# Moving the first layer's activations by one 64-byte line against the weights, with alternating output groups

## The chip, the cores and the metric

The kernel runs on one core of one Trainium2 chip, in one launch. The metric is device time in microseconds (us), the median of several runs. One further execution was recorded by the hardware profiler; its page and trace are what the text reads. Engines are named as the profile names them: PE (matmuls), PEld (loading the stationary operand, the weights), DVE, ACT, POOL, and SP, which issues most DMAs.

## The reference, cut to what matters

A two-layer encoder over 272 tokens (16 learned ones and 256 of the input), 2048 channels wide. Nearly all of its time is in products of the activations with large float32 weight matrices:

```python
for i in range(DEPTH):                      # 2 layers
    h = _rmsnorm(h_stream, norm_mix[i])
    proj = h @ w_in[i]                      # q, k, v, f and the two gates
    ...                                     # attention, 2-D Fourier branch
    a_br = attn @ w_attn_br[i]
    s_br = fr.reshape(B, L, FOURIER_WIDTH) @ w_four[i]
    merged = g_attn * a_br + g_four * s_br
    h_stream = h_stream + merged @ w_out[i]
    h2 = _rmsnorm(h_stream, norm_ffn[i])
    up = h2 @ w_up[i]
    u_gate = _dwconv3_centred(up[..., :D_FF], w_conv[i], b_conv[i])
    u_val = up[..., D_FF:]
    h_stream = h_stream + (jax.nn.silu(u_gate) * u_val) @ w_down[i]
```

## The kernel before, in words

Activations lie transposed in on-chip memory: 128 channels on the partitions, the 272 tokens (`T`) along the row. A product is taken in two-part arithmetic. Each float32 number is split into a high part and a low part, the rest. For each block of 128x128 weights PE does three matmuls into the same accumulator:

- L372: high weights (`wh`) with high activations
- L373: the same `wh` with low activations
- L374: low weights (`wl`) with high activations

In the first layer each of these streams 272 columns, in the second most stream 258 (the first 14 tokens are no longer needed; k and v still take 272).

`group` (L352 on) makes 256 output channels as two accumulators in PSUM, `m` = 0 and 1 (the "two output groups"). Its weights come in chunks of 512 KB: four blocks of contraction (`c` = 0 to 3) by two blocks of output. A list `cm` holds the eight pairs (c, m) of a chunk. Unsorted, m changes fastest: each block of activations is used for m = 0, then for m = 1, and the two accumulators alternate. Sorted by m, the chunk's four blocks go to m = 0 first and then to m = 1. Before, the first layer sorts every chunk, and the second layer only the last chunk of a group. The very first groups, f0 and f1, have code of their own (`first_groups`, L415 on, matmuls L439 to L441), which always alternates m.

Weights go by DMA into `raw`, ACT rounds them to `wh` (L307), DVE takes the difference `wl` (L309), two chunks ahead of their use. Results leave PSUM through DVE and ACT. Four accumulators of tag "mm" exist, so that one group may be emptied while the next is computed.

**Addresses.** All of these are 4-byte words along one partition's row. Call 16 words (64 bytes) a line. A token row has 272 = 17 x 16 words, so that each next block of activations (kt) starts one line later, modulo four lines; and the weights' rows are 272 words apart too (`CS = T`), so that each next c also starts one line later. The distance between the weights of a block and its activations, modulo 64 words, is then the same for all c and kt. What sets it are the offsets in the table of constants (L64 to L69), added to the place of each tile in the program's memory map:

| operand | place of the tile, mod 64 | offset before | start before, mod 64 |
|---|---|---|---|
| weights `wh`, `wl`, c = 0 | 32 | | 32 |
| `xHL` layer 0, high / low | 32 | 11 / 7 | 43 / 39 |
| `gHL` (into w_down), high / low | 48 | 59 / 55 | 43 / 39 |
| `mH` / `mL` (into w_out) | 0 / 0 | 43 / 39 | 43 / 39 |
| `q1` / `q2` (attention's output), high / low | 48 / 40 | 59 / 63 | 43 / 39 |
| `xHL` layer 1, 258 columns, high / low | 32 | 61+14 / 57+14 | 43 / 39 |
| `xHL` layer 1, 272 columns (k and v), high / low | 32 | 61 / 57 | 29 / 25 |

So in the first layer the highs start 11 words into the line in which the weights of the same block start (both modulo four lines), and the lows 4 words before the highs. `LOW = 60` makes the low part's distance: 60 is 4 short of 64.

Which weights are loaded beside which stream matters below: while PE streams a matmul, the weights of the next one are loaded. Beside L372 that is `wh` again, for L373; beside L373 it is `wl` of the same block; beside L374 it is the next block's `wh`: the same c with the other m, or the next c.

Of the kernel before, what the change touches and what calls it, by code (L numbers as in the profile page):

```python
# [20 lines left out]
T = NM + SEQ  # L21
DEPTH = 2
KT = D // P
# [11 lines left out]
FF_SPLIT = (24, 20)  # L35
# [25 lines left out]
TAIL_ORDER = (2, 3, 0, 1)  # L61
F0 = 1536
CS = T
LOW = 60  # L64
X_PAD, X_AT = 192, (11, 61)
G_AT, G_PAD = 59, 128
M_AT, M_PAD = ((43, 39), (21, 17)), (60, 22)
Q_AT, Q_PAD = (((59,), (63,)), ((61, 45), (57, 57))), (((76,), (84,)), ((62, 46), (62, 62)))
A_PAD, O_AT = 48, 16  # L69

def _branch(text):
# [91 lines left out]
def encoder_kernel(ctx, tc, xT, params, consts, bmat, cfold, csign, w_fl, w_f64c, w_in, w_abr, w_four, w_f64, w_out, w_up, w_down, w_vn, w_dn, w_dt, out):  # L163
# [13 lines left out]
    for l in range(DEPTH):  # L177
        def g(w, mg, k0, k1):
            return [(w[l, mg, c], CW) for c in range(k0 // CW, k1 // CW)]
# [11 lines left out]
        for half in range(2):  # L191
            for kind, j in BRANCH_ORDER[half]:
                w, off, n = {"ga": (w_in, IN_GA, KT), "gf": (w_in, IN_GF, KT), "s": (w_four, 0, 8), "a": (w_abr, 0, 8)}[kind]
                chs = [(fw[KT + 2 * j + c], CW) for c in range(2)] if (l, kind) == (1, "s") else g(w, off + j, 0, n)
# [19 lines left out]
    def due(t):  # L214
        (t0, d0), (t1, d1) = next(v for v in zip(DUE, DUE[1:]) if v[0][0] <= t < v[1][0])
        return d0 + (d1 - d0) * (t - t0) // (t1 - t0)

    chunks, folded, streamed, mix, summed, stage, small_w = [], set(), set(), {}, {}, {}, {}
    t, done = 0, 0
    for key, chs in order:  # L220
        for j, ch in enumerate(chs):
            n = 0
            if key[0] == 1 and key[1] in ("t", "ug", "uv"):
                n = due(t) - done
# [57 lines left out]
    def pump(upto=None):  # L282
        if upto is None:
            if todo:
                todo.pop(0)[1]()
        while upto is not None and todo and todo[0][0] <= upto:
            todo.pop(0)[1]()
# [32 lines left out]
    def step(force=False):  # L320
        if not force and slow[1] and slow[2]:
            slow[0] -= 1
            if slow[0] <= 0:
                slow[0] = slow[2]
                if next(slow[1], None) is None:
                    slow[1] = None
        for s in shadow:
            s[0] -= 1
        for s in list(shadow):
            if force or s[0] <= 0:  # L330
                try:
                    s[0] = next(s[1])
                except StopIteration:
                    shadow.remove(s)
                return
# [9 lines left out]
    def next_split():  # L345
        i = st["next"]
        advance(i + 1 + LOOK)
        pump(i)
        st["next"] += 1
        return splits.pop(i)  # L350

    def group(key, rhs, width, tag="mm"):  # L352
        k, chs = order[st["grp"]]
        assert k == key, (k, key)
        st["grp"] += 1
        nm = "_".join(str(v) for v in key)
        ps = [psum.tile([P, 512], F32, tag=tag, name=f"ps_{nm}_{m}") for m in range(MG)]
        nk = CW * len(chs)
        for j in range(len(chs)):
            for _ in range(mix.get((key, j), 0)):  # L360
                next(st["products"])
            h, lo = next_split()
            cm = [(c, m) for c in range(CW) for m in range(MG)]
            if key[0] == 0 or j == len(chs) - 1:
                cm.sort(key=lambda v: v[1])
            for n, (c, m) in enumerate(cm):
                kt = CW * j + c
                x = rhs(kt)
                sl = slice(m * P, (m + 1) * P)
                o = ps[m][:, :width]  # L370
                a, b = x
                nc.tensor.matmul(o, h[:, c, sl], a, start=kt == 0, stop=False)  # L372
                nc.tensor.matmul(o, h[:, c, sl], b, start=False, stop=False)  # L373
                nc.tensor.matmul(o, lo[:, c, sl], a, start=False, stop=kt == nk - 1)  # L374
                if n % 2:
                    step()
                    pump()
        return ps
# [73 lines left out]

    XT = per.tile([P, KT, T], F32, name="XT")
    xf = per.tile([P, KT * 2 * T + X_PAD], F32R, name="xHL")
    xHLs = [xf[:, o:o + 2 * (KT * T + LOW)].rearrange("p (r x) -> p r x", r=2)[:, :, :KT * T].rearrange("p r (k t) -> p r k t", k=KT) for o in X_AT]
    xHL, xH, xL = xHLs[0], xHLs[0][:, 0], xHLs[0][:, 1]
    prm = per.tile([P, P_N], F32, name="prm")
    cst = per.tile([P, C_N], F32, name="cst")
# [71 lines left out]
    def norm_in(m, goff):  # L530
        norm_split(m, goff)
        norm_sum(m)
# [96 lines left out]
    for l in range(DEPTH):  # L629
# [7 lines left out]
        with tc.tile_pool(name=f"mix{l}", bufs=1) as mp:  # L637
# [105 lines left out]
            if l == 0:  # L743
# [19 lines left out]
                with tc.manual_schedule(engines={mybir.EngineType.PE, mybir.EngineType.DVE}):  # L763
                    ps = group((l, "f", 2), xr(0), T, "aux")
# [7 lines left out]
                tc.keep_in_program_order(nc.vector.tensor_tensor(br3[64:96], brem[32:64], br3[32:64].bitcast(F32), op=ALU.subtract))  # L772
                tc.keep_in_program_order(nc.vector.tensor_scalar(bgh, prm[:, P_BG:P_BG + DEPTH * 2 * KT], 0.5, None, op0=ALU.mult))
                f_evac(3, group((l, "f", 3), xr(0), T))
            else:
                push(norm_stats(hold), 8)
# [413 lines left out]
            for i in range(4):  # L1190
# [3 lines left out]
                if last:  # L1194
                    if i in (0, 2):
                        until(hold, "vt" if i == 0 else "fold")
                        for t_, n in ((qH, "q1"), (qL, "q2")):
                            o = Q_AT[l][t_ is qL][i // 2]
                            t = mp.tile([P, 4 * T + Q_PAD[l][t_ is qL][i // 2]], F32R, tag=n + "ab"[i // 2], name=n)
                            t_.append(t[:, o:o + 4 * T].rearrange("p (h t) -> p h t", t=T))  # L1200
                elif i == 0:
                    until(hold, "vt")
                    until(hold, "fold")
                    for t_, n in ((qH, "q1"), (qL, "q2")):
                        o = Q_AT[l][t_ is qL][0]
                        t = mp.tile([P, NH * T + Q_PAD[l][t_ is qL][0]], F32R, tag=n, name=n)[:, o:o + NH * T].rearrange("p (h t) -> p h t", t=T)
# [26 lines left out]
            for half in range(2):  # L1233
                mH = mL = None
                for n_, (kind, i) in enumerate(BRANCH_ORDER[half]):
                    if half or last and n_ >= 4:
                        slow[2] = 22
                    j = i - 4 * half
# [18 lines left out]
                    else:  # L1257
# [7 lines left out]
                        for m in range(MG):  # L1265
                            k = 2 * j + m
# [14 lines left out]
        with tc.tile_pool(name=f"ffn{l}", bufs=1) as fp:  # L1281
# [6 lines left out]
            def conv_gate(i):  # L1288
                ps = group((l, "ug", i), xr(lo), W)
                until(hold, "tok2")  # L1290
                cs = []
                for m in range(MG):
                    mt = 2 * i + m
                    wc = lambda t: prm[:, P_CW + (l * 3 + t) * FT + mt:P_CW + (l * 3 + t) * FT + mt + 1]
                    bc = prm[:, P_CB + l * FT + mt:P_CB + l * FT + mt + 1]
                    u = fp.tile([P, T], F32, tag="u", name="u", bufs=3)
                    nc.vector.tensor_tensor(u[:, lo:T], ps[m][:, :W], rstdB[:, lo:T], op=ALU.mult)
                    cv = fp.tile([P, T], F32, tag="cv", name="cv", bufs=4)
                    nc.scalar.activation(cv[:, lo2:T], u[:, lo2:T], AF.Identity, bias=bc, scale=wc(1))
                    a = max(lo2, 1)  # L1300
                    nc.vector.scalar_tensor_tensor(cv[:, a:T], u[:, a - 1:T - 1], wc(0), cv[:, a:T], op0=ALU.mult, op1=ALU.add)
                    nc.vector.scalar_tensor_tensor(cv[:, lo2:T - 1], u[:, lo2 + 1:T], wc(2), cv[:, lo2:T - 1], op0=ALU.mult, op1=ALU.add)
                    nc.scalar.activation(cv[:, lo2:T], cv[:, lo2:T], AF.Silu)
                    if not last:
                        nc.vector.tensor_tensor(cv, cv, rstdB, op=ALU.mult)
                    cs.append(cv)
                return cs

            def split_to(h, low, v):
                nc.scalar.copy(h, v)  # L1310
                nc.vector.tensor_tensor(low, v, h.bitcast(F32), op=ALU.subtract)

            k0 = 0
            for c, n in enumerate(() if last else FF_SPLIT):
                gf = fp.tile([P, FF_SPLIT[0] * 2 * T + G_PAD], F32R, tag="gHL", name="gHL")
                gH, gL = (gf[:, G_AT + (FF_SPLIT[0] * T + LOW) * r:G_AT + (FF_SPLIT[0] * T + LOW) * r + FF_SPLIT[0] * T].rearrange("p (k t) -> p k t", t=T) for r in range(2))
                for i in range(k0 // MG, (k0 + n) // MG):
                    cs = conv_gate(i)
                    ps = group((l, "uv", i), xr(0), T)
                    for m in range(MG):  # L1320
                        j = 2 * i + m - k0
                        nc.vector.tensor_tensor(cs[m], cs[m], ps[m][:, :T], op=ALU.mult)
                        split_to(gH[:, j], gL[:, j], cs[m])
                for mg in range(8):
                    ps = group((l, "d", c, mg), lambda kt: (gH[:, kt], gL[:, kt]), T)
                    for m in range(MG):
                        mt = 2 * mg + m
                        nc.vector.tensor_tensor(XT[:, mt], XT[:, mt], ps[m][:, :T], op=ALU.add)
                        if c == len(FF_SPLIT) - 1:
                            norm_in(mt, P_NM + (l + 1) * KT)  # L1330
                k0 += n
            if last:
# [152 lines left out]
                for i in UP_ORDER:  # L1485
# [16 lines left out]
                    for m in range(0 if i in VPAIRS else MG):  # L1502
                        j = 2 * i + m
# [19 lines left out]
                for b in TAIL_ORDER:  # L1523
                    k, chs = order[st["grp"]]
# [95 lines left out]
```

## Time and profile before

| | us |
|---|---|
| median of 3 runs | 2483.73 (2483.13 to 2485.19) |
| the profiled execution | 2484.18 |
| its span, first to last instruction | 2482.4 |
| layer 0 (to the first k group of layer 1) | 0 to 1301.3 |
| of that, w_in, attention, Fourier branch and w_out | 0 to 522.6 |
| of that, w_up and w_down | 522.6 to 1301.3 |

The time of the profiled execution is 1.8 us above its span, and 0.45 us above the median. On the page, PE and PEld are two parts of one engine that overlap; matmuls are pipelined, so that the record of one lasts more than twice as long as the step from its start to the next one's start. Where speed is meant, the steps are to be read, not the records' lengths.

### The profile page before, as it was taken

How to read it: one execution, taken by the hardware profiler on the slowest of the kernel's cores; microseconds unless marked ns; L12 is line 12 of the kernel's file. 1: busy time of each engine (PE TensorE's matmuls, PEld its weight loads, DVE VectorE, ACT ScalarE, POOL GpSimd, SP SyncE). 2: the span in 40 equal slices, each digit the busy share in tenths (PEclk: the TensorE clock that was granted, in tenths of full speed). 3: DMA queues.
4: the chain of work that ended last, by engine and by line, in shares of the span. 5: the costliest groups of instructions: out<-in, count | busy, mean ns of one | idle time of the engine just before them, and what ended most of it. 6: DMA issues, size and time to landing. Idle time of an engine off the chain costs nothing.

```text
span 2482.4 us, 48288 instructions
## 1 busy us (share of the span) xinstructions
PE 2473.8 (100%) x19040; PEld 2401.3 (97%) x19040; DVE 1984.1 (80%) x3143; ACT 1335.9 (54%) x1901; POOL 205.0 (8%) x394
## 2 busy tenths in 40 slices
PE   9999999999999999999999999999999999999999
PEld 9999999999999999999999999999998899988987
DVE  7687866778878767888778887666878787898898
ACT  5455534554444334444445655444676665676665
POOL 0000000012212222222210000000000000000000
PEclk9999999999999999999999999999999999999999
DMA  7545557879999999999986647888888887888887
GB/s 249 170 154 165 192 195 245 271 256 376 403 326 387 404 386 385 395 384 396 396 296 201 198 159 245 271 266 274 254 271 296 299 291 237 264 283 296 281 303 271
DMA packets 194805, 706.88 MB, mean 285 GB/s; under 512 B 22145, under 2 KB 27393, under 8 KB 194321
## 3 DMA queue, kind: packets, MB, share of 16 engines
q1 hardware_dynamic: 146768, 517.09, 60.3%
q0 software_dynamic: 46368, 184.57, 21.3%
q8 instruction: 149, 2.44, 0.4%
q10 hardware_dynamic: 1440, 2.13, 0.2%
q14 instruction: 80, 0.65, 0.1%
HBM read 623.32 MB, written 111.15 MB: 296 GB/s over the span
## 4 chain that ended last, share of the span: by engine, by line
PE 99%; DMA 0%; DVE 0%; issue 0%; ACT 0%; POOL 0%; DVEq 0%; ACTq 0%; POOLq 0%
PE ps_p L1462 14%; PE ps_ug L372 7%; PE ps_ug L374 7%; PE ps_ug L373 7%; PE ps_uv L372 4%; PE ps_uv L374 4%; PE ps_uv L373 4%; PE ps_d L372 4%; PE ps_d L374 3%; PE ps_d L373 3%; PE ps_gf L372 3%; PE ps_ga L372 2%; PE ps_o L372 2%; PE ps_ga L374 2%; PE ps_gf L374 2%; PE ps_o L374 2%
## 5 line engine op out<-in xcount | busy, mean ns | idle before, releaser
L307 ACT CAST wh<-raw 128x1024 fp32r<-128x1024 f32 (+1 forms) x961 | 997.7, 1043 | 873.1 <-PE ps_ug L373 211.6
L309 DVE TENSOR_TENSOR wl<-raw,wh 128x1024 fp32r<-128x1024 f32 (+1 forms) x961 | 1158.6, 1218 | 386.2 <-ACT wh L307 375.1
L372 PE MATMUL ps_ug<-xHL,wh 128*128 128x272 f32 (+1 forms) x1408 | 397.9, 283 | 0.0
L374 PE MATMUL ps_ug<-xHL,wl 128*128 128x272 f32 (+1 forms) x1408 | 394.3, 281 | 0.2 <-DVE wl L309 0.2
L373 PE MATMUL ps_ug<-xHL,wh 128*128 128x272 f32 (+1 forms) x1408 | 394.5, 280 | 0.0
L373 PEld LDWEIGHTS ps_ug<-xHL,wh 128*128 128x128 f32 x1408 | 264.8, 188 | 3.2
L372 PEld LDWEIGHTS ps_ug<-xHL,wh 128*128 128x128 f32 x1408 | 264.3, 188 | 3.3
L374 PEld LDWEIGHTS ps_ug<-xHL,wl 128*128 128x128 f32 x1408 | 263.7, 188 | 1.5 <-DVE wl L309 1.1
L372 PE MATMUL ps_uv<-xHL,wh 128*128 128x272 f32 (+1 forms) x896 | 254.9, 285 | 0.0
L374 PE MATMUL ps_uv<-xHL,wl 128*128 128x272 f32 (+1 forms) x896 | 252.2, 282 | 0.3 <-DVE wl L309 0.3
L373 PE MATMUL ps_uv<-xHL,wh 128*128 128x272 f32 (+1 forms) x896 | 252.5, 282 | 0.0
L1462 PE MATMUL ps_p<-wh,opnd 128*128 128x512 f32 x816 | 221.8, 393 | 0.0
L372 PE MATMUL ps_d<-gHL,wh 128*128 128x272 f32 x704 | 201.3, 286 | 0.0
L373 PE MATMUL ps_d<-gHL,wh 128*128 128x272 f32 x704 | 199.2, 283 | 0.0
L374 PE MATMUL ps_d<-gHL,wl 128*128 128x272 f32 x704 | 198.9, 283 | 0.0
L1462 PEld LDWEIGHTS ps_p<-wh,opnd 128*128 128x128 f32 x816 | 148.1, 188 | 28.6
L373 PEld LDWEIGHTS ps_uv<-xHL,wh 128*128 128x128 f32 x896 | 168.9, 188 | 0.8
L374 PEld LDWEIGHTS ps_uv<-xHL,wl 128*128 128x128 f32 x896 | 168.0, 188 | 1.0 <-DVE wl L309 1.0
L372 PEld LDWEIGHTS ps_uv<-xHL,wh 128*128 128x128 f32 x896 | 168.2, 188 | 0.8
L535 DVE TENSOR_TENSOR wi<-wi,wi 128x512 f32<-128x512 f32 x224 | 147.2, 685 | 0.1
L372 PE MATMUL ps_ga<-xHL,wh 128*128 128x272 f32 (+1 forms) x512 | 146.5, 286 | 0.0
L372 PE MATMUL ps_gf<-xHL,wh 128*128 128x272 f32 (+1 forms) x512 | 145.4, 284 | 0.0
(375 smaller groups left out, 5776.1 us busy)
## 6 DMA issues: line engine op xcount, KB each, us to landing
raw<-in_w_up SPq DMA_DIRECT2D x288, 512.0 KB, 6.6
raw<-in_w_in SPq DMA_DIRECT2D x191, 512.0 KB, 4.2
raw<-in_w_down SPq DMA_DIRECT2D x88, 512.0 KB, 7.2
wi<-in_w_dn POOLq DMA_DIRECT2D x80, 512.0 KB, 9.7
ft<-wi POOLq DMA_DIRECT2D x80, 512.0 KB, 7.8
raw<-ft SPq DMA_DIRECT2D x80, 512.0 KB, 4.7
raw<-in_w_out SPq DMA_DIRECT2D x64, 512.0 KB, 4.4
raw<-fv SPq DMA_DIRECT2D x64, 512.0 KB, 4.7
```

The lines of the kernel that those rows point to most:

```text
L307: nc.scalar.copy(h[:, a:b], r[:, a:b])
L309: nc.vector.tensor_tensor(lo[:, a:b], r[:, a:b], h[:, a:b].bitcast(F32), op=ALU.subtract)
L372: nc.tensor.matmul(o, h[:, c, sl], a, start=kt == 0, stop=False)
L373: nc.tensor.matmul(o, h[:, c, sl], b, start=False, stop=False)
L374: nc.tensor.matmul(o, lo[:, c, sl], a, start=False, stop=kt == nk - 1)
L535: tt = lambda *v, **kw: tc.keep_in_program_order(nc.vector.tensor_tensor(*v, **kw))
L1462: nc.tensor.matmul(ps[h], x, w[:, 512 * h:512 * h + 512], start=fresh and (s_, q) in BEGIN and first, stop=(s_, q) in END and end, skip_gr ...
```

## The change

Two things, in the first layer alone. (1) The high activations start one line earlier (27 instead of 43, modulo 64), so that the weights of the same block start in the line after them, 5 words on; the lows start 4 words after the highs (31) instead of 4 before. This holds for all four kinds of operand, `xHL`, `gHL`, `mH`/`mL` and `q1`/`q2`. (2) `group` doesn't sort a chunk in the first layer any more, not the last one either: the two accumulators alternate in every chunk. The second layer keeps its addresses and its order.

```diff
-LOW = 60
-X_PAD, X_AT = 192, (11, 61)
-G_AT, G_PAD = 59, 128
-M_AT, M_PAD = ((43, 39), (21, 17)), (60, 22)
-Q_AT, Q_PAD = (((59,), (63,)), ((61, 45), (57, 57))), (((76,), (84,)), ((62, 46), (62, 62)))
+LOW = (4, 60)
+X_PAD, X_AT = 192, (59, 61)
+G_AT, G_PAD = 43, 128
+M_AT, M_PAD = ((27, 31), (21, 17)), (60, 22)
+Q_AT, Q_PAD = (((43,), (55,)), ((61, 45), (57, 57))), (((76,), (84,)), ((62, 46), (62, 62)))
...
-            if key[0] == 0 or j == len(chs) - 1:
+            if key[0] == 1 and j == len(chs) - 1:
                 cm.sort(key=lambda v: v[1])
...
-    xHLs = [xf[:, o:o + 2 * (KT * T + LOW)].rearrange("p (r x) -> p r x", r=2)[:, :, :KT * T].rearrange("p r (k t) -> p r k t", k=KT) for o in X_AT]
+    xHLs = [xf[:, o:o + 2 * (KT * T + n)].rearrange("p (r x) -> p r x", r=2)[:, :, :KT * T].rearrange("p r (k t) -> p r k t", k=KT) for o, n in zip(X_AT, LOW)]
...
-                gH, gL = (gf[:, G_AT + (FF_SPLIT[0] * T + LOW) * r:G_AT + (FF_SPLIT[0] * T + LOW) * r + FF_SPLIT[0] * T].rearrange("p (k t) -> p k t", t=T) for r in range(2))
+                gH, gL = (gf[:, G_AT + (FF_SPLIT[0] * T + LOW[0]) * r:G_AT + (FF_SPLIT[0] * T + LOW[0]) * r + FF_SPLIT[0] * T].rearrange("p (k t) -> p k t", t=T) for r in range(2))
```

On PE, the first chunk of the first w_down group (tiles `ps_d_0_0` and `ps_d_0_1` are its accumulators m = 0 and 1, three rows to a block). Before:

```order
L372 MATMUL ps_d_0_0_10286<-gHL,wh_10223 128x272
L373 MATMUL ps_d_0_0_10286<-gHL,wh_10223 128x272
L374 MATMUL ps_d_0_0_10286<-gHL,wl_10224 128x272
L372 MATMUL ps_d_0_0_10286<-gHL,wh_10223 128x272
L373 MATMUL ps_d_0_0_10286<-gHL,wh_10223 128x272
L374 MATMUL ps_d_0_0_10286<-gHL,wl_10224 128x272
```

and now, at the same place:

```order
L372 MATMUL ps_d_0_0_10286<-gHL,wh_10223 128x272
L373 MATMUL ps_d_0_0_10286<-gHL,wh_10223 128x272
L374 MATMUL ps_d_0_0_10286<-gHL,wl_10224 128x272
L372 MATMUL ps_d_0_1_10287<-gHL,wh_10223 128x272
L373 MATMUL ps_d_0_1_10287<-gHL,wh_10223 128x272
L374 MATMUL ps_d_0_1_10287<-gHL,wl_10224 128x272
```

Before, the accumulator stays m = 0 for the chunk's four blocks of contraction; now it changes after every third matmul, and the weights loaded beside L374 are every other time those for m = 1 of the same c. The count of matmuls is the same.

On DVE, the last group of attention's output projection (a7) and the start of the second half of w_out (`ps_o`): L1268 and L1269 take `ps_a` out of PSUM and add the other branch, L1271 writes `mL`, which the w_out group reads. Before:

```order
L309 TENSOR_TENSOR wl_6092<-raw_5907,wh_6091 128x4x256
L1268 SCALAR_TENSOR_TENSOR th<-th,ps_a_0_6048 128x272
L1269 TENSOR_TENSOR th<-th 128x272
L1268 SCALAR_TENSOR_TENSOR th<-th,ps_a_1_6049 128x272
L1269 TENSOR_TENSOR th<-th 128x272
L309 TENSOR_TENSOR wl_6132<-raw_5940,wh_6131 128x4x256
L1271 TENSOR_TENSOR mL<-th,mH 128x272 x2
```

and now:

```order
L309 TENSOR_TENSOR wl_6092<-raw_5907,wh_6091 128x4x256
L1268 SCALAR_TENSOR_TENSOR th<-th,ps_a_0_6048 128x272
L1268 SCALAR_TENSOR_TENSOR th<-th,ps_a_1_6049 128x272
L1269 TENSOR_TENSOR th<-th 128x272 x2
L309 TENSOR_TENSOR wl_6132<-raw_5940,wh_6131 128x4x256
L1271 TENSOR_TENSOR mL<-th,mH 128x272 x2
```

The same instructions stand there; only the two halves of the emptying are interleaved, because both accumulators now become ready at nearly the same time. POOL's and SP's rows are the same as before.

## The prediction

> **What bounds the kernel now.** I read the page first: busy shares, and the chain that ended last.
>
> ```profile
> span 2482.4 us, 48288 instructions
> PE 2473.8 (100%) x19040; PEld 2401.3 (97%) x19040; DVE 1984.1 (80%) x3143; ACT 1335.9 (54%) x1901; POOL 205.0 (8%) x394
> ...
> PE 99%; DMA 0%; DVE 0%; issue 0%; ACT 0%; POOL 0%; DVEq 0%; ACTq 0%; POOLq 0%
> ```
>
> PE is never free and the chain is PE from end to end. Next, what PE waited for:
>
> ```profile
> engine line waited for: us in total, times, longest us
> PE ps_f L439 <- ACT wh L307: 4.4, 1, 4.4
> PE ps_uv L374 <- DVE wl L309: 0.3, 1, 0.3
> PE ps_ug L374 <- DVE wl L309: 0.2, 1, 0.2
> ```
>
> These are 4.9 us in all, so nothing is to be had from waits. The time is a count of matmuls times the step from one start to the next. The count of the first layer, from the windows view of line L372 up to layer 1, and of L439:
>
> ```profile
> 0.00:1301.30 1301.30, 937.74 (x3264) 612.88 (x3265) 1.00 0.84 306
> ...
> 0.00:1301.30 1301.30, 19.91 (x64) 13.03 (x64) 1.00 0.84 306
> ```
>
> That is 3,328 triples (L372 to L374, or L439 to L441), 9,984 matmuls of 272 columns. One nanosecond on each is 10 us, and a whole 0.2% of the time, about what a measurement of this kernel can tell from no change, is 5.0 us or 0.5 ns on each. The clock in these rows is 1.00, so no throttle hides in the step.
>
> **The step, and what it depends on.** The first half of w_down, groups by line, then one row of the tile view with first and last start:
>
> ```profile
> L372 PE MATMUL ps_d<-gHL,wh 128*128 128x272 f32 x384 | 109.8, 286 | 0.0
> L373 PE MATMUL ps_d<-gHL,wh 128*128 128x272 f32 x384 | 108.7, 283 | 0.0
> L374 PE MATMUL ps_d<-gHL,wl 128*128 128x272 f32 x384 | 108.5, 283 | 0.0
> ...
> L374 PE MATMUL ps_d<-gHL,wl x384: 282/283/283, 806.6 to 947.6; 128*128 128x272 f32 x192
> ```
>
> From 806.6 to 947.6 lie 383 triples: 368.1 ns a triple, 122.7 ns a step. The three records are 285.9, 283.1 and 282.6 ns (busy by count), 851.6 together; so a record is 161.1 ns longer than its step on average ((851.6 - 368.1) / 3), and with that constant the steps are 124.8, 122.0 and 121.5. The matmuls are alike but for the addresses, so the kinds must differ by what is read beside them. The timeline shows it: the next weights are loaded from the moment a stream starts.
>
> ```profile
> 899.99 0.28 PE L373 MATMUL ps_d<-gHL,wh 128*128 128x272 f32 x1
> 899.99 0.19 PEld L374 LDWEIGHTS ps_d<-gHL,wl 128*128 128x128 f32 x1
> ...
> 900.11 0.28 PE L374 MATMUL ps_d<-gHL,wl 128*128 128x272 f32 x1
> 900.12 0.19 PEld L372 LDWEIGHTS ps_d<-gHL,wh 128*128 128x128 f32 x1
> ```
>
> Beside L372 the weights start in the same line as the highs (modulo four lines): the dear kind, 285.9. Beside L374, in the sorted order, they are the next c's, one line further, 5 words past the start of the highs: the cheap kind, 282.6. That both stand at third place as well is seen in f0 and f1, which alternate at the same addresses, so that L441 has the same line every other time:
>
> ```profile
> L441 PE MATMUL ps_f<-xHL,wl x33: 282/286/392, 19.8 to 31.9; 128*128 128x272 f32 x33
> L439 PE MATMUL ps_f<-xHL,wh x32: 285/286/286, 19.9 to 31.7; 128*128 128x272 f32 x32
> L440 PE MATMUL ps_f<-xHL,wh x32: 283/283/286, 20.1 to 31.8; 128*128 128x272 f32 x32
> ```
>
> L441 is 282 or 286: same line 286, one line on 282, at the same place in the triple and with the same stream. This is the pair on which the forecast rests.
>
> **The change part by part.** *Highs one line back.* Beside L372 the weights now start one line on, 5 words past the highs, as they did beside L374. Its record should go from 285.9 to 282.6: -3.3 ns a triple.
>
> *Alternation.* Beside L374 the weights are half the time the same c's: again 5 words on, 282.6, no change. Half the time they are the next c's, now two lines on. No row of 272 columns shows that distance. Its bounds are the two kinds seen, 282.6 and 285.9; no row is nearer to the one than to the other, since same line and two lines lie one line to either side of the cheap place; I take the dear one: +3.3 ns in half the triples, +1.7 a triple. With the cheap one it would be 0, another 5.7 us off the sum (1.7 x 3,328).
>
> *Lows.* No row shows the new distance, 1 word, either. Put the loaded weights at word 32 in each case: the streams seen then start at 27 (L374, 282.6), 39 (L373, 283.1) and 43 (L372, 285.9), all at word 3 of a group of four, as the new lows are. The new start, 31, lies between the first two. The bounds are 282.6 (-0.5) and 285.9 (+2.8); I take 283.1, no change.
>
> *Sum.* -3.3 + 1.7 + 0 = -1.6 ns a triple; times 3,328 is **-5.3 us**. All of it is on the path, since PE sets the end. The two unknown places together reach from -1.6 - 1.7 - 0.5 = -3.8 ns a triple (-12.6 us) to -1.6 + 2.8 = +1.2 ns (+4.0 us).
>
> *The later accumulator.* Without sorting, m = 0 is ready 9 matmuls or 1.1 us later (9 x 0.1227), near the group's end. The tightest place is a7 into w_out:
>
> ```profile
> L373 PE MATMUL ps_o<-mL,wh x40: 283/283/283, 475.6 to 490.0; 128*128 128x272 f32 x40
> ...
> 474.89 0.43 DVE L1268 SCALAR_TENSOR_TENSOR th<-th,ps_a 128x272 f32<-128x272 f32 x1
> ...
> 477.79 0.79 DVE L1271 TENSOR_TENSOR mL<-th,mH 128x272 fp32r<-128x272 f32 x2
> ...
> 479.30 0.28 PE L373 MATMUL ps_o<-mL,wh 128*128 128x272 f32 x1
> ```
>
> The two `mL` are done at about 478.2 and 478.6; the first reader of the first is the L373 at 479.30 (third block of the second chunk), 1.1 us later. w_out's first L373 stands at 475.6, so a7 ended near 475.5; its m = 0 had ended 1.5 us before that (12 steps), but DVE took it up only at 474.89. Now it can do so near 475.3, 0.4 us later. The reader moves by more: in alternating order the third block of a chunk stands after 12 matmuls, not 6, 0.74 us later. So cost 0; the cover is the chunk that stands between. If it were gone, each of some six hand-overs (f, q, a twice, the two w_down) would lose up to 1.1 us, 6.6 us.
>
> **A rule of the skill against it.** In the Trainium skill, "TensorE: Matmul & The Clock Gate", section "Step-by-step: what each phase is for", says that PE has two independent read ports, and that loading the next weights takes no bandwidth from the running matmul. By that, relative addresses could not matter and the sum would be 0. The 282 and 286 of L441 speak against it, and more so the k rows below, where the same three lines step by 129 ns.
>
> **The rivals.**
>
> *No gain (slightly slower).* The lows pay: 1 word past their start may collide where 5 words don't. At 285.9 they cost +2.8 ns, the sum becomes +1.2 ns a triple, +4.0 us: 2487.7. It decides from 284.7, where the gain is used up. For it: 1 word is nearer than any seen; against it: its place between two cheap starts. Chance 0.19.
>
> *Two free ports.* If the 3 ns had another cause than the addresses, such as the repeated `wh`, distance would be free, the triple would stay at 368.1, and the time at 2483.7. Against it stands L441. Chance 0.04. (It is what the rule above of the Trainium skill's "TensorE: Matmul & The Clock Gate" would give.)
>
> *Not the distance, but the change of block (slower).* Where L441 is cheap, the next stream is another block of activations, too; where it is dear, the next one reads the same block again. If that is the cause, L372 stays at 285.9, L374 becomes dear in half the triples, and a dear third matmul also makes a following L440 dear (283 to 286 in its row). The price stands in f0 and f1, which run just so:
>
> ```profile
> 24.15 0.28 PE L441 MATMUL ps_f<-xHL,wl 128*128 128x272 f32 x1
> ...
> 27.86 0.28 PE L441 MATMUL ps_f<-xHL,wl 128*128 128x272 f32 x1
> ```
>
> 30 steps in 3.71 us, 123.7 ns against 122.7: 1.0 ns on 9,792 matmuls (f0 and f1 have it already), +9.8 us, 2493.5. It decides if L372 stays above some 284 ns, where what it saves no longer pays for the alternation (285.9 - 1.7). Against it: L372's own next stream is another one, the lows, and it is dear. Chance 0.13.
>
> *The streams lose their phase.* In layer 1, k and v read 272 columns from 29 and 25, which also puts the weights in the next line, 3 and 7 words on:
>
> ```profile
> 1303.79 0.29 PE L373 MATMUL ps_k<-xHL,wh 128*128 128x272 f32 x1
> ...
> 1305.99 0.29 PE L372 MATMUL ps_k<-xHL,wh 128*128 128x272 f32 x1
> ```
>
> 17 steps in 2.20 us, 129.4 ns: 6.7 ns dearer, +67 us over 9,984 matmuls, 2550. By line alone this is the nearest place to the new one. Against it: these starts are word 1 of a 16-byte group, while all well-running ones, and the new ones, are word 3. Chance 0.11.
>
> *All cheap.* Every record at 282.6 is -3.8 ns a triple, -12.6 us: 2471.1. The second layer agrees roughly:
>
> ```profile
> L374 PE MATMUL ps_o<-mH,wl x126: 276/277/278, 1588.5 to 1632.0; 128*128 128x258 f32 x126
> ...
> L1541 PE MATMUL ps_t<-wh,t 128*128 128x512 f32 x56 | 17.1, 390 | 0.0
> ...
> L1541 PE MATMUL ps_t<-wh,t 128*128 128x256 f32 x8 | 1.6, 281 | 0.0
> ```
>
> 125 triples in 43.5 us are 116.0 ns a step at 258 columns; a column costs (390 - 281) / 256 = 0.43 ns, so 14 more make 122.0, -0.7 ns on 9,984, -7 us. Chance 0.18.
>
> That the change doesn't do what it says is excluded: PE's rows alternate in every first-layer group, and the starts follow from the offsets.
>
> **How the numbers follow.** The execution profiled took 2484.18, 0.45 over the median; -5.3 gives 2478.9 in its own time and **2478.4** as a median. The forecast (-8 to -3 us, 2475.5 to 2480.5) has 0.35, of which 0.06 lies within 5.0 us of the old time. Faster by over 0.2%: 0.29 + 0.18 = 0.47. Within: 0.06 + 0.19 + 0.04 = 0.29. Slower: 0.13 + 0.11 = 0.24. The range reaches from the cheapest sum, 2471, rounded out to 2470 for the ends of that case, to 2494, which takes in the change of block; it leaves out the lost phase (0.11) and some hundredths at the low end.
>
> **What would show it.** L372 of `ps_d` at 282 to 283 instead of 286: the high step right; at 286, distance is not what counts. L374 with two values, 282 and 286: the alternation as reckoned; one value of 282: the cheap rival. L373 tells the lows: 283, or 286. The first half of w_down, 141 us from first to last start, should take 140.4; 142 is the change of block, 149 the lost phase. Records spread over many values are the lost phase too. A PE wait on `mL`, `gL` or `xHL` would make the hand-over wrong. Layer 1 should keep its 1,181 us.

## The result and the profile after

| | median of 9 runs, us | profiled execution, us | its span, us |
|---|---|---|---|
| before | 2484.29 (2483.12 to 2485.31) | 2484.18 | 2482.4 |
| after | 2490.86 (2489.92 to 2493.01) | 2493.01 | 2491.2 |

After / before is 1.0027, 95% interval 1.0017 to 1.0038: **slower by 6.6 us**, where 5.3 us less was forecast. The page of the kernel after, busy times and the chain that ended last:

```profile
span 2491.2 us, 48303 instructions
PE 2481.9 (100%) x19040; PEld 2409.8 (97%) x19040; DVE 1983.0 (80%) x3143; ACT 1335.1 (54%) x1901; POOL 203.4 (8%) x394
...
PE 99%; DMA 0%; DVE 0%; issue 0%; ACT 0%; POOL 0%; DVEq 0%; ACTq 0%; POOLq 0%
```

The bound is the same, and so is the count of matmuls. PE's waits after:

```profile
PE ps_f L439 <- ACT wh L307: 5.1, 2, 4.4
PE ps_uv L374 <- DVE wl L309: 0.3, 1, 0.3
PE ps_ug L374 <- DVE wl L309: 0.2, 1, 0.2
```

No new wait has come, so the time is again count by step. Where the first layer grew is read from the tile view's first and last starts: the first k matmul and the last one of w_down. Before, then after:

```profile
L372 PE MATMUL ps_k<-xHL,wh x64: 286/288/491, 59.5 to 1314.1; 128*128 128x272 f32 x64
L374 PE MATMUL ps_d<-gHL,wl x704: 282/283/283, 806.6 to 1301.2; 128*128 128x272 f32 x176
```

```profile
L372 PE MATMUL ps_k<-xHL,wh x64: 283/288/491, 61.5 to 1322.8; 128*128 128x272 f32 x64
L374 PE MATMUL ps_d<-gHL,wl x704: 283/283/288, 811.9 to 1309.9; 128*128 128x272 f32 x176
```

From 59.5 to 1301.2 are 1241.7 us; from 61.5 to 1309.9 are 1248.4. These +6.7 us are as much as the medians differ (6.6); the other 2.0 us of the profiled execution lie ahead of the first k matmul, in the opening stretch, where the first k matmul stood anywhere from 58.3 to 60.3 us in the kernels below. Behind the last w_down row nothing changed (2482.4 - 1301.2 = 1181.2; 2491.2 - 1309.9 = 1181.3). The first half of w_down, grouped by line (busy us, mean ns), and then in the tile view (shortest, median, longest; first and last start):

```profile
L373 PE MATMUL ps_d<-gHL,wh 128*128 128x272 f32 x384 | 109.7, 286 | 0.0
L372 PE MATMUL ps_d<-gHL,wh 128*128 128x272 f32 x384 | 109.6, 285 | 0.0
L374 PE MATMUL ps_d<-gHL,wl 128*128 128x272 f32 x384 | 108.7, 283 | 0.0
```

```profile
L372 PE MATMUL ps_d<-gHL,wh x384: 283/284/287, 811.7 to 953.7; 128*128 128x272 f32 x192
L373 PE MATMUL ps_d<-gHL,wh x384: 284/284/288, 811.8 to 953.8; 128*128 128x272 f32 x192
L374 PE MATMUL ps_d<-gHL,wl x384: 283/283/288, 811.9 to 953.9; 128*128 128x272 f32 x192
```

From 811.9 to 953.9 are 142.0 us, against 141.0 before and 140.4 forecast: 370.8 ns a triple against 368.1. (Below, a triple's price is the mean over a stage, taken from the starts in the trace to the nanosecond and good to some 0.1 ns; such rows check it roughly.) L372's record fell only from 285.9 to 285.4 ns, and L373's rose from 283.1 to 285.7. L374, which was to carry the price of the alternation, rose by half a nanosecond. The timeline shows why:

```profile
899.79 0.28 PE L374 MATMUL ps_d<-gHL,wl 128*128 128x272 f32 x1
899.92 0.29 PE L372 MATMUL ps_d<-gHL,wh 128*128 128x272 f32 x1
900.04 0.29 PE L373 MATMUL ps_d<-gHL,wh 128*128 128x272 f32 x1
900.17 0.28 PE L374 MATMUL ps_d<-gHL,wl 128*128 128x272 f32 x1
900.29 0.28 PE L372 MATMUL ps_d<-gHL,wh 128*128 128x272 f32 x1
900.41 0.28 PE L373 MATMUL ps_d<-gHL,wh 128*128 128x272 f32 x1
900.54 0.28 PE L374 MATMUL ps_d<-gHL,wl 128*128 128x272 f32 x1
```

The load beside the L374 at 899.79 is the next c's, two lines on: its own record is short, and the L372 and L373 behind it are long. The load beside the one at 900.17 is the same c's, 5 words on, and the next two are short. L372 has the same pair of addresses in both places and two prices. **A step is not set by its own pair alone.**

### The profile page after: what moved, and what is told of

It is laid out like the page before. It is cut to its first block, busy times and chain, and to the rows that moved or that the text cites. A ratio compares the mean times of both kernels' runs of the same rounds, so it can differ in the third digit from the quotient of the medians.

```text
span 2491.2 us, 48303 instructions
## 1 busy us (share of the span) xinstructions
PE 2481.9 (100%) x19040; PEld 2409.8 (97%) x19040; DVE 1983.0 (80%) x3143; ACT 1335.1 (54%) x1901; POOL 203.4 (8%) x394
## 4 chain that ended last, share of the span: by engine, by line
PE 99%; DMA 0%; DVE 0%; issue 0%; ACT 0%; POOL 0%; DVEq 0%; ACTq 0%; POOLq 0%
PE ps_p L1462 14%; PE ps_ug L372 7%; PE ps_ug L374 7%; PE ps_ug L373 7%; PE ps_uv L372 4%; PE ps_uv L373 4%; PE ps_uv L374 4%; PE ps_d L372 4%; PE ps_d L373 4%; PE ps_d L374 3%; PE ps_gf L372 2%; PE ps_ga L372 2%; PE ps_o L372 2%; PE ps_o L373 2%; PE ps_gf L373 2%; PE ps_ga L373 2%
## 5 line engine op out<-in xcount | busy, mean ns | idle before, releaser
L372 PE MATMUL ps_ug<-xHL,wh 128*128 128x272 f32 (+1 forms) x1408 | 397.5, 283 | 0.0
L373 PE MATMUL ps_ug<-xHL,wh 128*128 128x272 f32 (+1 forms) x1408 | 396.3, 282 | 0.0
L374 PE MATMUL ps_ug<-xHL,wl 128*128 128x272 f32 (+1 forms) x1408 | 394.8, 281 | 0.2 <-DVE wl L309 0.2
L373 PEld LDWEIGHTS ps_ug<-xHL,wh 128*128 128x128 f32 x1408 | 264.2, 188 | 3.3
L372 PEld LDWEIGHTS ps_ug<-xHL,wh 128*128 128x128 f32 x1408 | 264.1, 188 | 3.3
L374 PEld LDWEIGHTS ps_ug<-xHL,wl 128*128 128x128 f32 x1408 | 264.4, 188 | 1.5 <-DVE wl L309 1.3
L372 PE MATMUL ps_uv<-xHL,wh 128*128 128x272 f32 (+1 forms) x896 | 254.5, 284 | 0.0
L373 PE MATMUL ps_uv<-xHL,wh 128*128 128x272 f32 (+1 forms) x896 | 254.4, 284 | 0.0
L374 PE MATMUL ps_uv<-xHL,wl 128*128 128x272 f32 (+1 forms) x896 | 252.6, 282 | 0.3 <-DVE wl L309 0.3
L373 PE MATMUL ps_d<-gHL,wh 128*128 128x272 f32 x704 | 201.1, 286 | 0.0
L372 PE MATMUL ps_d<-gHL,wh 128*128 128x272 f32 x704 | 200.9, 285 | 0.0
L374 PE MATMUL ps_d<-gHL,wl 128*128 128x272 f32 x704 | 199.3, 283 | 0.0
L374 PEld LDWEIGHTS ps_uv<-xHL,wl 128*128 128x128 f32 x896 | 168.8, 189 | 1.0 <-DVE wl L309 1.0
L373 PEld LDWEIGHTS ps_uv<-xHL,wh 128*128 128x128 f32 x896 | 168.3, 188 | 0.8
L372 PEld LDWEIGHTS ps_uv<-xHL,wh 128*128 128x128 f32 x896 | 168.0, 187 | 0.8
L372 PE MATMUL ps_ga<-xHL,wh 128*128 128x272 f32 (+1 forms) x512 | 146.2, 286 | 0.0
L372 PE MATMUL ps_gf<-xHL,wh 128*128 128x272 f32 (+1 forms) x512 | 145.2, 284 | 0.0
```

## The experiments

A cell is written highs/lows (where the two start, modulo 64 words, with the weights of the same block put at 32) and order. A load is so many words on when its weights start that many words, modulo 64, behind the start of the stream that runs beside it. Before is 43/39 sorted, after 27/31 alternating. Three theories at first: *carry* (the load beside the third matmul decides, and is paid for by the rows behind it), *distance alone* (each pair has its price, as predicted), *order alone* (alternating costs, wherever the streams start).

**One part undone.** The new addresses with the old order, and the old addresses with the new order.

```diff
-            if key[0] == 1 and j == len(chs) - 1:
+            if key[0] == 0 or j == len(chs) - 1:
```

is e1, made on the kernel after, and

```diff
-            if key[0] == 0 or j == len(chs) - 1:
+            if key[0] == 1 and j == len(chs) - 1:
```

is e2, made on the kernel before.

> The new addresses with the old order (every first-layer chunk sorted by output group). In the changed kernel a triple of matmuls takes 370.8 ns in w_up and w_down, against 368.3 before; in its trace the L372 and L373 after an L374 that loads weights two lines on step 125 and 126 ns, those after an L374 that loads 5 words on step 122.5 and 123.5. Theory 'carry': a load two lines on leaves the next two matmuls dear; sorted, every L374 is of that kind, so the triple becomes 122.5 + 125.2 + 125.8 = 373.5 ns, and the time about 9 us over the changed kernel, 2500. Theory 'distance alone' (that of the prediction, with the changed kernel's mean steps): L372 123.6, L373 124.3, L374 122.8, the triple stays at 370.8, 2491. Theory 'order alone': the addresses matter nothing and only alternation costs, so the triple returns to 368.3 and the time to 2484.

> The old addresses with the new order (no first-layer chunk sorted). Groups f0 and f1, which always alternate, take 371.0 ns a triple at the old addresses and 370.8 at the new. Theory 'carry' and theory 'order alone': all first-layer groups take 371.0, +2.7 ns on 3264 triples, 2493. Theory 'addresses alone' (the order costs nothing, the new distances do): 368.3, 2484.

Measured: e1 2501.68 us (ratio 1.0071, 1.0057 to 1.0084), e2 2491.77 us (1.0033, 1.0021 to 1.0044), against 2483.66. The first half of w_down in the tile view, e1 and then e2:

```profile
L372 PE MATMUL ps_d<-gHL,wh x384: 284/287/287, 816.2 to 959.5; 128*128 128x272 f32 x192
L373 PE MATMUL ps_d<-gHL,wh x384: 284/287/288, 816.3 to 959.6; 128*128 128x272 f32 x192
L374 PE MATMUL ps_d<-gHL,wl x384: 283/285/285, 816.4 to 959.7; 128*128 128x272 f32 x192
```

```profile
L372 PE MATMUL ps_d<-gHL,wh x384: 285/286/286, 810.3 to 952.3; 128*128 128x272 f32 x192
L373 PE MATMUL ps_d<-gHL,wh x384: 283/284/286, 810.4 to 952.4; 128*128 128x272 f32 x192
L374 PE MATMUL ps_d<-gHL,wl x384: 282/284/286, 810.5 to 952.5; 128*128 128x272 f32 x192
```

That is 143.3 and 142.0 us. The two parts in one table (triple in ns, median of runs in us):

| | 43/39 | 27/31 |
|---|---|---|
| sorted | 368.3, 2483.7 to 2484.3 (before) | 374.0, 2501.7 (e1) |
| alternating | 370.8, 2491.8 (e2) | 370.8, 2490.9 (after) |

Moving the activations gains nothing in the new order and costs 5.7 ns in the old one; alternating costs 2.5 ns at the old place and saves 3.2 at the new one. Distance alone (2491 for e1) and order alone (2484 for e1) are both out; carry came near both.

**Other cells.** Two kernels with a cell of their own in each stage of the first layer, sorted in some groups and alternating in others. On the kernel after, the offsets of e3 (e4 has others):

```diff
-LOW = (4, 60)
-X_PAD, X_AT = 192, (59, 61)
-G_AT, G_PAD = 43, 128
+LOW = (4, 60, 4, 60)
+X_PAD, X_AT = 192, (11, 61, 59, 61)
+G_AT, G_LOW, G_PAD = (43, 59), (12, 52), 128
...
-            if key[0] == 1 and j == len(chs) - 1:
+            if j == len(chs) - 1 if key[0] else key[1] in ("ug", "ga") or key[1] in ("d", "o", "q") and key[-1] % 2 == 0:
```

> Six layouts in one kernel, read stage by stage from the steps; highs/lows are starts modulo 64 words with the weights of the block at 32. w_up 27/31 (ug sorted, uv alternating); first half of w_down 27/39, second half 43/31, first w_out half 27/23, second 43/39 (in these even groups are sorted, odd ones alternate); the gates 43/47 (ga sorted, gf alternating). Theory 'carry': sorting makes 27/31 dearer (373.5 against 370.8 ns a triple) and 43/39 cheaper (368.3 against 371); 27/39, whose L374 loads two lines on as well, behaves like 27/31, sorted dearer than alternating; 43/31, whose L374 loads 5 words on when sorted, like 43/39. Theory 'the low parts cost it' (1 word past the lows' start collides): 27/39 and 27/23 fall to 368 or below in alternating order, 43/31 rises by about 2 ns when sorted. Theory 'order alone': every layout is 368.3 sorted and 371 alternating.

> Six further layouts, the same orders in the same stages: w_up 59/63, first half of w_down 59/55, second half 11/7, first w_out half 11/15, second 27/35, the gates 43/35. Theory 'carry': what counts is the distance at L374 in the loop's order. Sorted it loads the next block one line on from the same block's distance; for 11/7 and 11/15 the same block is two lines on and the next three, which is like one and two lines if the pattern repeats after two lines: 11 sorted then is as 43 sorted (368), 59 as 27 (373). Theory 'four lines count': no pair agrees. Any layout below 368 in either order would be a better version than both kernels.

Measured: 2495.66 and 2500.22 us, one run each; by stage, ns a triple:

| cell | sorted | alternating | | cell | sorted | alternating |
|---|---|---|---|---|---|---|
| 43/39 (w_out) | 368.3 | 370.8 | | 27/35 (w_out) | 374.9 | 372.7 |
| 43/31 (w_down) | 371.7 | 372.5 | | 11/15 (w_out) | 375.2 | 372.2 |
| 27/31 (w_up) | 373.9 | 370.8 | | 11/7 (w_down) | 375.0 | 374.1 |
| 27/23 (w_out) | 374.0 | 370.6 | | 59/55 (w_down) | 375.0 | 374.2 |
| 27/39 (w_down) | 374.9 | 370.9 | | 59/63 (w_up) | 375.0 | 374.1 |

In the new order the lows are not the cause: at 23, 31 and 39 the triple is 370.6 to 370.9. Two more cells, read from the last three groups of each gate, are 43/47 and 43/35: 374.0 sorted for both, and 370.7 and 371.0 alternating. So with the highs at 43 and sorted, where the load beside the third matmul is always 5 words on, the triple takes 368.3, 371.7 or 374.0 by the lows. But prices don't add up either: lows at 31 instead of 39 cost 3.4 ns with the highs at 43 (368.3 to 371.7), and save 1.0 with the highs at 27 (374.9 to 373.9), both sorted.

**Order and distance apart.** With weights' rows 256 words apart and activations' rows 320 (both multiples of 64), the load beside the third matmul has the same distance whatever comes next; so order can be changed with the distances held. That was done in w_out; other stages ran a chunk's blocks backwards (c = 3 to 0). In the diff of e5 (e6 has other cells) the second edit makes the weights dense.

```diff
+M_AT, M_PAD, M_T = (((27, 31), (43, 39)), ((21, 17), (21, 17))), (448, 22), (320, 272)
...
+            if key[:2] in ((1, "t"), (0, "o")):
...
+            if key[0] == 0 and key[1] in ("uv", "d"):
+                cm = [(CW - 1 - c, m) for c, m in cm]
+            if j == len(chs) - 1 if key[0] else not (key[1] in ("d", "o") and key[-1] % 2):
```

> One run with a different cell in each stage of layer 0; what is read is the time of a triple (first to last start of a stage over its triples), by group. 'Reversed' means that a chunk's four blocks run c = 3 to 0, so that the next block's weights lie a line back. In w_out the rows of the activations are 320 words apart and the weights' 256, so that the distance of streams and weights is the same beside the first and the third matmul, whatever the order. Third-matmul theory (the triple is cheap when the weights loaded beside the third matmul start 5 words on, whatever lies beside the first): w_up gate, 43/39 sorted as in the kernel before, 368.3; w_up value, 43/39 sorted reversed (third: 37 on) 374; w_down first half 27/31 reversed, sorted groups (third: same line) 374, alternating groups 371; w_down second half 11/7 reversed, sorted groups (third: 5 on, first: 21 on) 368.3, alternating 371; w_out first half 27/31, 5 on everywhere, 368 in sorted and in alternating groups; w_out second half 43/39, same line everywhere, 374 in both. Distance by pairs, as predicted: w_down first half 368.3 sorted, second half cheap only at the third; w_out first half 365 in both orders, second half 371.6. Order alone: every sorted group 368.3, every alternating one 370.8, whatever the distance. If no cell but the control is at 368.3, the cheap case belongs to the combination of place and ascending order and not to a distance.

> As the run beside it, other cells. w_up gate 11/15 sorted reversed (first 21 on, third 5 on); w_up value 11/15 alternating reversed; w_down first half 59/55 reversed (first 37 on, third 21 on); w_down second half 27/23 reversed (first 5 on, third same line); w_out with equal distances 27/23 in the first half and 27/39 in the second. Third-matmul theory: w_up gate 368.3, w_up value 371; w_down first half 374 or more in both orders, second half 374 sorted and 371 alternating; w_out 368 in both halves and both orders. Distance by pairs: w_up gate 371 to 372 (dear at the first matmul only), w_out 365. Order alone: sorted 368.3, alternating 370.8. A cell below 368 would be a layout that beats both kernels.

Measured: e5 2489.83 us and e6 2486.11, one run each. The first halves of w_out in the two kernels, third matmul (L376 here; two lines were added above):

```profile
L376 PE MATMUL ps_o<-mH,wl x128: 282/285/288, 318.0 to 364.9; 128*128 128x272 f32 x128
```

```profile
L376 PE MATMUL ps_o<-mH,wl x128: 282/283/283, 317.4 to 363.9; 128*128 128x272 f32 x128
```

46.9 us against 46.5 for 127 triples. The finer means, in ns:

| w_out, equal distances | words on beside the 1st, 2nd, 3rd | sorted | alternating |
|---|---|---|---|
| 27/31 (e5) | 5, 1, 5 | 370.0 | 370.0 |
| 43/39 (e5) | 53, 57, 53 | 373.3 | 373.3 |
| 27/23 (e6) | 5, 9, 5 | 366.6 | 366.7 |
| 27/39 (e6) | 5, 57, 5 | 368.9 | 368.9 |

With the distances held, the order costs nothing. The carry theory falls here too: it wanted 368 wherever the load beside the third matmul is 5 words on. 11/15 backwards in sorted order, which has that, did run at 368.4, but 11/7 backwards, which has it as well, at 371.7, no better than 43/39 backwards (371.7), which has not; and 27/31 above is at 370.0. And here the lows pay: 31 against 23 is +3.4 ns. What is left I call *joint distance*: the three distances set the triple together, and the order acts through them alone. It also gives e2's mean: half its triples have 53 beside the third, half have 5, and (373.3 + 368.3) / 2 = 370.8, as measured. The trace of e2 has no triple of 373 or 368 ns, though: each takes 370 or 371. In the first half of w_down the step beside the same-line load is 124.2 ns instead of 121.7, and the second step of the next triple 125.0 instead of 122.4: one load is paid for in two triples.

As a rule for a single triple, joint distance is refuted by the starts in the traces. In e1 every triple has the same three distances modulo 64 words (5, 1 and 21), and it has two prices: 375.0 ns in most, but 368.3 in the fifth of every chunk's eight, for which the streams go back to the chunk's first block, and in the first of a group. Rows of e1 from the end of a chunk's fourth triple on:

```profile
817.57 0.28 PE L374 MATMUL ps_d<-gHL,wl 128*128 128x272 f32 x1
817.70 0.28 PE L372 MATMUL ps_d<-gHL,wh 128*128 128x272 f32 x1
817.82 0.28 PE L373 MATMUL ps_d<-gHL,wh 128*128 128x272 f32 x1
817.94 0.28 PE L374 MATMUL ps_d<-gHL,wl 128*128 128x272 f32 x1
818.07 0.29 PE L372 MATMUL ps_d<-gHL,wh 128*128 128x272 f32 x1
818.19 0.29 PE L373 MATMUL ps_d<-gHL,wh 128*128 128x272 f32 x1
818.32 0.28 PE L374 MATMUL ps_d<-gHL,wl 128*128 128x272 f32 x1
...
819.57 0.29 PE L372 MATMUL ps_d<-gHL,wh 128*128 128x272 f32 x1
```

From 817.70 to 818.07 are 0.37 us, and the four triples from 818.07 to 819.57 take 1.50, 375 ns each. In e5's 27/31 with equal distances the triples take about 368 and 372 ns in turn, in both orders alike; 370.0 is their mean. So equal distances made the order free in every cell tried, but distances modulo 64 words do not fix a triple's price by themselves.

**A version from it.** 27/23 with equal distances is 1.7 ns below the kernel before. There is no room for rows of 320 words everywhere, so e7 first put the four blocks of a chunk at places of one phase, and moved the chunk's weights along; only the last triple of a chunk has another distance. e8 and e9 try further cells in that layout.

```diff
+BLOCK_AT = [T * (4 * (k % 4) + -(k // 4) % 4) if k < 16 else 16 * T + (2 * T + 32) * (k % 4) + T * (k // 4 % 2) for k in range(24)]
...
+                w_at[len(chunks)] = BLOCK_AT[4 * (0 if key[1] == "o" else j // 2 if key[1] == "f01" else j)] % 64
...
-            return w[:, :CW * MG * P].rearrange("p (c m) -> p c m", c=CW)
+            return w[:, o:o + CW * MG * P].rearrange("p (c m) -> p c m", c=CW)
```

> The kernel before in its sorted order, with all three loads of a triple held at one distance: highs at 27, lows at 23, weights' rows 256 words apart, the activation blocks of one chunk at places of one phase (modulo 64 words) and the chunk's weights moved by the same phase. The load beside every stream starts 5 or 9 words on, but for the last triple of each chunk (1 in 8), whose third load is the next chunk's, one line back. Attention's output projection keeps 43/39. Joint-distance theory (the distances of the three loads set the triple together, the order acts through them alone; prices from the two w_out halves and the w_down half of the runs before: 366.6 with 5 everywhere, 371.6 with the third load one line back): 7/8 x 366.6 + 1/8 x 371.6 = 367.3 ns a triple, 366.6 in w_out; about -1.1 ns on 2,944 triples and -1.7 on 256, -3.6 us: near 2480. Prices by pair, as predicted (each record at 282.6 or 283.1): 365 ns, -10 us, 2474. Order alone: 368.3, 2483.7. The places of blocks have no price of their own in any of them; if they have, it comes out slower.

> Equal distances as in the run beside it, with the next chunk's weights one line on at the chunk's end, other cells: w_in and w_up highs 31, lows 27 (loads 1 and 5 words on); w_down 23 and 19 (9 and 13 on); w_out 27 and 19 (5 and 13 on). Joint-distance theory has no price for these cells; it expects sorted triples on the ladder of 1.67 ns (366.6, 368.3, 370.0, 371.7, 373.3) mixed with 1/8 of some 374, not all alike. Prices by pair: 366 to 368 everywhere, since all loads lie in the next line. A cell under 366 would make a better layout.

> As the run beside it: w_in and w_up 27 and 19 (5 and 13 words on), w_down 27 and 27 (5 and 5 on), w_out 27 and 7 (5 and 25 on). Joint-distance theory: steps of the same ladder; 27/27 tells whether highs and lows at one phase are better than 4 words apart. Prices by pair: 365 for 27/27, the others by their lows alone.

Measured: e7 2482.10 us against 2483.47, ratio 0.9993 (0.9984 to 1.0002): no difference that can be told. Its w_out, with no end of chunk that differs, is at 366.67 as expected; w_up and w_down are at 367.9 to 368.1, not 367.3. One disturbed triple in eight costs (368.1 - 366.7) x 8 = 11 ns, more than the 5 ns by which the disturbed cell itself is dearer: again a price that reaches into the triples behind. In w_up the last triple of a chunk takes 369 ns and the next three 371, 367 and 371. e8 took 2498.21 us: 31/27 372.7, 23/19 373.5, 27/19 371.7. e9 took 2490.85: 27/19 371.5, 27/27 370.2, and 27/7 in w_out 366.7, as good as 27/23. All of these but the lows at 7 are loads in the next line, and they differ by up to 7 ns (366.7 to 373.5).

27/7 leaves room between highs and lows. So e10 lays a block's highs and lows side by side in a row of 576 words, nine times 64; all blocks of w_in, w_up and w_down then have one phase, ends of chunks included. w_out gets 27/23, with another distance at the end of a chunk. `_Blocks` looks a block up in such a list of places. e11 is e10 in the change's order, which is the last edit.

```diff
+PAIR = 2 * T + 32
+PAIR_LOW = T + 28
+PAIR_AT = [PAIR * k for k in range(24)]
...
-                gH, gL = (gf[:, G_AT + (FF_SPLIT[0] * T + LOW) * r:G_AT + (FF_SPLIT[0] * T + LOW) * r + FF_SPLIT[0] * T].rearrange("p (k t) -> p k t", t=T) for r in range(2))
+                gH, gL = (_Blocks(gf[:, G_AT + r * PAIR_LOW:], PAIR_AT) for r in range(2))
...
-            if key[0] == 0 or j == len(chs) - 1:
+            if key[0] == 1 and j == len(chs) - 1 or key[:2] == (0, "a"):
```

> A version meant to beat both kernels: the kernel before in its sorted order, with the blocks of high and low activations side by side in rows of 576 words (272 high, 28 free, 272 low, 4 free), so that every block of every chunk has the same phase, and dense weights (256 words a row). In w_in, w_up and w_down all highs start at 27 and all lows at 7, weights put at 32: 5 and 25 words on beside every stream, at the ends of chunks too; w_out 27 and 23 with one changed distance at the end of each chunk; f0 and f1 get it as well; attention's output projection and the second layer keep their distances. Joint-distance theory (the 27/7 and 27/23 halves of w_out measured 366.67): 366.7 ns a triple, -1.66 ns on 2,880 triples, -1.1 on 256, -4.3 on 64: -5.4 us, 2478.1. If the end of a chunk or the place of the blocks is what counts, no gain: 2482 or more. Prices by pair, as predicted: the lows at 25 words on have no row; with 283 for them 365.0 ns, -10 us.

> The run beside it with the change's order: the two output groups alternate in every chunk of the first layer (attention's output projection stays sorted). Distances are the same in both orders. Joint-distance theory: the same triples, 366.7 ns, and the same time within 1 us, so that the order has no price but through distances. Order alone: +2.5 ns a triple as at the old addresses, +7.8 us.

Measured, against 2483.52 for the kernel before: e10 **2478.80 us** (ratio 0.9980, 0.9972 to 0.9989), e11 2478.67 (0.9981, 0.9971 to 0.9990). Busy times on the page of e10:

```profile
span 2476.7 us, 48288 instructions
PE 2467.8 (100%) x19040; PEld 2395.8 (97%) x19040; DVE 1983.5 (80%) x3143; ACT 1335.6 (54%) x1901; POOL 202.9 (8%) x394
```

The first half of w_down in the tile view, e10 and then e11 (L392 is the third matmul there):

```profile
L392 PE MATMUL ps_d<-gHL,wl x384: 283/283/288, 802.9 to 943.3; 128*128 128x272 f32 x192
```

```profile
L392 PE MATMUL ps_d<-gHL,wl x384: 283/283/288, 803.4 to 943.8; 128*128 128x272 f32 x192
```

Both take 140.4 us, 366.7 ns a triple by the finer mean, in w_up too; w_out is at 367.4 in both. So the alternation that costs 8.1 us at the old addresses (e2) costs nothing here.

## Why the prediction was wrong

- **The bound, the count, the cover**: right. PE ends the span, the 9,984 matmuls are the same, layer 1 keeps its 1,181 us, and no wait on `mL`, `gL` or `xHL` came with the later accumulator.
- **The step that failed: "Highs one line back", -3.3 ns a triple.** In the change's own order the move is worth 0.0 ns (e2 to after, 370.8 and 370.8), in the old order it costs 5.7 (before to e1). Behind it stands the reading that the dear record belongs to its own pair, "285.9 beside the same line, 282.6 one line on", and that prices add up over the three matmuls. They don't: the table below has the steps themselves, the lows' move from 39 to 31 costs 3.4 ns with one place of the highs and saves 1.0 with the other, and in the timeline of the kernel after the same L372 has two prices. The pair L441, on which the forecast was said to rest, was a correct reading of a record, but L441 is one part of a triple whose other parts move with it: as a whole, the triples of its two kinds are 368.3 ns (before) and 373.3 (e5), 5.0 apart and not 3.3, because half of the price falls on a later matmul (e2).

  Mean steps in the first half of w_down, in ns, from the starts in the traces (after: third to eighth triple of each chunk):

  | | L372 | L373 | L374 | triple |
  |---|---|---|---|---|
  | before | 124.25 | 122.42 | 121.67 | 368.3 |
  | after, behind a load 5 words on | 122.58 | 123.33 | 122.42 | 368.3 |
  | after, behind a load 21 words on (two lines) | 125.00 | 125.92 | 122.42 | 373.3 |

  For the kernel before, the prediction's constant had put the steps at 124.8, 122.0 and 121.5. Behind a load 5 words on, L372 saves 1.7 ns and not 3.3, and L373 and L374 give it all back. The load two lines on costs 5.0 ns, all of it in the two matmuls behind.
- **Alternation, +1.7**: right in sign, mis-sized; +2.5 at the old place (e2). With the highs' 0.0 that makes +2.5 ns, which is what w_up, w_down, w_out and attention's output projection show after (370.8, against 368.3): 2,496 triples, 6.2 us. The other 704 triples between the first k matmul and layer 1, those of w_in, lie among other matmuls and rose by less: 6.7 us were read from the starts above, which leaves them some 0.5 us together.
- **Lows, 0**: right for the triple in the change's order (370.6 to 370.9 for 23, 31 and 39), wrong as a general price: +3.4 ns for 31 against 23 where the distances are equal (e6 to e5).
- **The rivals.** "The lows pay" (2487.7) and "change of block" (2493.5) both ended on the right side. The second came nearest, because it took its price from rows that ran in just that order, f0 and f1: 123.7 ns a step, and e2 gives 370.8 / 3 = 123.6. It asked that L372 stay above 284 ns, and at 285.4 it did. As a general reason it is out all the same: in e11 every block is read twice in a row as well, at no price. The lost phase, 149 us for half of w_down, didn't occur; it was 142.0. "All cheap" (-3.8 ns a triple, 2471.1) came nowhere: the cheapest stages of all kernels are at 366.7 ns. That e10 there has just the forecast's -1.6 ns, with other lows and equal distances, is chance.
- **Two free ports.** By the rule quoted there from the Trainium skill, "TensorE: Matmul & The Clock Gate", section "Step-by-step: what each phase is for", the triple would be the same in all these kernels. It runs from 366.7 to 375.2 ns with addresses and order alone, so the trace speaks against it.

Open: what makes the addresses count. That the streams and the loads disturb each other is inferred from the prices; no row shows it. Mixing the two kinds of triples half and half gives 43/39 (370.8) and nearly 27/23 (366.7 and 374.0 make 370.4; measured 370.6), but not after's own cell: 370.0 and 374.0 make 372.0, and its triples take 368.3 and 373.3 in turn, 370.8. No rule that gives a cell's price ahead of a run came out of this.

## What to carry to other kernels

When a loop of matmuls is paced by its own steps, price the whole repeating unit, as it will stand, from first and last starts; a record's length tells neither which operation caused it nor what is saved when that one changes. If no unit like the new one has run, the forecast has no price, and rows that ran in nearly that order are a better estimate than a sum of pairs. Where streams and weights may be placed freely, give the rows of both a stride that is a multiple of 64 words, so that every load has the same distance, and measure a few places. That the strides are equal is not enough: with 272 words for both, as before and after, the next block's weights lie a line further. Nor are equal distances without the place: e8 and e9 have them in at least seven of eight triples of most stages and took 2498.2 and 2490.9 us. Here e10's place was worth 4.7 us, and its layout made the order free.

## What was not expected of the hardware

- Most stages that kept to one cell lie, in the mean, on a ladder of 1.67 ns a triple, about four columns of the 0.43 ns that the prediction's rows give: 366.7 (27/23 and 27/7 equal), 368.3 (43/39), 370.0 (27/31 equal), 371.7 (43/31, 27/19 equal, five of the backwards cells), 373.3 (43/39 equal), 375.0 (11/7, 59/55, 59/63). Some means are made of unlike triples (27/31 equal: 368 and 372 in turn), and 27/39 equal (368.9) is off it.
- Matmuls that are alike but for addresses and order take from 366.7 to 375.2 ns for three, 2.3%, with a granted clock of 1.00 in all of these kernels; and a single load that lies otherwise is paid for by the matmuls behind it (e7's ends of chunks: 11 ns for one in eight triples).
